# Second-layer conditioning columns: 24 of 48 moved from TensorE in the first MLP to VectorE in the second layer's attention

## The chip, the cores and the metric

The kernel runs on one core of a Trainium2 chip. Its time is the device time of one execution in microseconds (us); the figure to predict is the median of several executions. The engines are TensorE (PE, with its weight loads PEld), VectorE (DVE), ScalarE (ACT), GpSimd (POOL) and SyncE (SP), which issues most of the DMAs.

## The reference, cut to what matters

A trunk of two layers on x of 512 x 1024. From the vector c each layer makes six conditioning vectors of 1024, which scale, shift and gate its two halves:

```python
c_act = jax.nn.silu(c)
for l in range(DEPTH):                                   # DEPTH = 2
    ada = c_act @ ada_w[l] + ada_b[l]                    # 1024 x 6144 per layer
    sh1, sc1, g1, sh2, sc2, g2 = jnp.split(ada, 6, axis=-1)
    h = modulate(x, sh1, sc1)
    y = even_mixer(h, ...) if l % 2 == 0 else diff_mixer(h, ...)
    x = layer_norm(ALPHA * x + (1.0 + g1[:, None, :]) * y, ln_g[l, 0], ln_b[l, 0])
    h = modulate(x, sh2, sc2)
    y = sq_relu_mlp(h, mlp_w1[l], mlp_w2[l])
    x = layer_norm(ALPHA * x + (1.0 + g2[:, None, :]) * y, ln_g[l, 1], ln_b[l, 1])
```

`diff_mixer` projects h to queries, keys and values for 8 heads, takes two causal softmaxes per head, subtracts them, multiplies by the values, normalises and projects out. `sq_relu_mlp` is `square(relu(h @ w1)) @ w2`. All is float32.

## The kernel before, in words

The kernel keeps a conditioning vector as columns of 128 values: layer l has 48 columns m, eight for each of the six vectors, in the tile `adac[:, l, m]`. Columns 0 to 23 are sh1, sc1 and g1; columns 24 to 47 are sh2, sc2 and g2, which are first needed behind the layer's attention. A column needs 512 KB of weights, and they come by one load, like every other weight block.

All weights pass through one `Stream`. It is a list of items in a fixed order, each with a source of 512 KB in DRAM. A free "raw" buffer is given to the next item in the list, and SyncE loads it. `process` works the items off in the same order and hands the raw buffer on. A weight item is split into a high and a low float32r part (ScalarE copies the high part, line 265, and VectorE or GpSimd subtracts, line 266), which needs a free "slot" for the result. A conditioning item needs no slot. `get(item)` processes all items up to the one wanted; `pump(n)` processes up to n if a slot is there. Matmuls use three products of high and low parts (lines 350 to 352).

A conditioning item is handled in `prepare`, in one of three ways. Where `ada_pe(l, m)` holds, two items make a pair on TensorE (`ada_pair`): 8 float32 matmuls with 32 equal weight columns (line 422; each takes two instructions), a scalar copy of the result, two matmuls that bring it into column form (line 427), and an addition of the bias. Otherwise VectorE multiplies the raw block with the activated c and sums along the row (line 250, one instruction and the read of its accumulator), or GpSimd multiplies and ScalarE sums (lines 247 and 248). Now all 48 columns of layer 1 go by TensorE, spread evenly by `some` over the items of layer 0's MLP (`mlp_items`), a new one after most of its weight items.

The order of the work is written out in Python; a scheduler then places the instructions on their engines by that order as a priority, and an instruction whose inputs and buffers are there may go ahead of an earlier one that waits.

Around the change, in order: layer 0's MLP. It runs 13 groups; a group makes seven products of the first matrix (`products`, one VectorE addition at line 913 each group) between eight units of the second (`gemm2`). Then the LN of layer 0 (`ln_a`, `ln_b`, VectorE, GpSimd, ScalarE and transposes), which writes the four accumulators to DRAM (`axd`) and frees them. Then `odd`, the second layer's attention. It first projects the values: two halves of 512 columns, each for four row tiles t, each a sum over four weight items `v half c` of two blocks (24 matmuls per half and row tile). The results go to two banks "mm" of PSUM in turn. A slot is freed when t = 3 has used it, and one `pump` follows each of these. There are five slots; v00 to v03 and v10 hold them while the first half runs. Then head by head: a projection of queries and keys (items `qk`), and the softmax pipeline over 32 units (line 1681 and following). In this stretch the stream has two raw buffers. Four buffers with the tag "u4" hold the accumulators; in `odd` two of them become `V`, and the others are first used again when the residual is read back from `axd` (line 1765). Behind the heads `layer` runs the output projection, the LN and the second MLP.

Of the kernel before, what the change touches and what calls it, by code (L numbers as in the profile page):

```python
# [9 lines left out]
F32 = mybir.dt.float32  # L10
# [96 lines left out]
class Stream:  # L107
# [130 lines left out]
    def prepare(self, it):  # L238
        k, nc = self.k, self.k.nc
        n = it.n  # L240
        raw = it.raw[0][:, :n]
        if it.ada is not None:
            l, m = it.ada
            if not k.ada_pe(l, m):
                acc = k.adac[:, l, m:m + 1]
                if bool(16 <= m < 48) != ((l, m) in PLAN["ax"]):
                    nc.gpsimd.tensor_tensor(out=raw, in0=raw, in1=k.cact, op=ALU.mult)
                    nc.scalar.activation(out=raw, in_=raw, func=AF.Copy, scale=0.5, accum_out=acc)
                else:
                    nc.vector.scalar_tensor_tensor(out=raw, in0=raw, scalar=0.5, in1=k.cact, op0=ALU.mult,  # L250
                                                   op1=ALU.mult, accum_out=acc)
            elif m % 2:
                k.ada_pair(l, m - 1, self.held.raw[0], raw)
        else:
            kind = [c for c in self.kinds(it) if self.slots[c]][0]
            it.slot, it.kind = self.slots[kind].pop(0), kind
            hi, lo = it.slot
            if it.scale is not None:
                g = it.scale()
                w = 1024  # L260
                for c in range(0, n, w):
                    (nc.vector if it.name in PLAN["sc"] else nc.gpsimd).tensor_tensor(out=raw[:, c:c + w], in0=raw[:, c:c + w], in1=g[:, c:c + w], op=ALU.mult)
            for c in hi.pieces(n, {}.get(k.phase, 1024)):
                w = c.stop - c.start
                nc.scalar.copy(out=hi.cols(c.start, w), in_=raw[:, c])  # L265
                getattr(nc, ("vector", "gpsimd")[PLAN["lo"][it.name]] if it.name in PLAN["lo"] else k.lo_engine).tensor_sub(out=lo.cols(c.start, w), in0=raw[:, c], in1=f32(hi.cols(c.start, w)))  # L266
# [60 lines left out]
class Trunk:  # L327
# [80 lines left out]

    def ada_pe(self, l, m):

        return l > 0 or m >= 40

    def ada_src(self, l, m):
        return self.a["ada_p"][8 + m if l else m - 40] if self.ada_pe(l, m) else self.a["ada_w"][m]

    def ada_pair(self, l, m, r0, r1):

# [333 lines left out]
    def mlp_items(self, l):  # L751
        a, st = self.a, self.st
        def ada(n, mark=None):
            for _ in range(min(n, len(left))):
                l2, m = left.pop(0)
                self.last_ada = st.add(self.ada_src(l2, m), ada=(l2, m))
                if mark:
                    self.last_ada.after = lambda: self.marks[mark]
# [10 lines left out]
            ada((0, 0, 0, 0, 8, 0, 0, 0)[f], None)  # L769
        if left or l == 0 and 16 < 24:  # L770
            self.gate_ada = self.last_ada
        left = [(1, m) for m in range(48 - sum((0, 0, 0, 0, 0, 0, 0, 0)))] if l == 0 else []
        p0, p1 = 8, 54
        count = [0]

        def some():
            count[0] += 1
            ada(len(left) - (48 - sum((0, 0, 0, 0, 0, 0, 0, 0))) * max(0, min(p1 - p0, p1 - count[0])) // (p1 - p0) if left else 0)
        self.xd[l] = [self.DR.tile([128, 1024], F32, name=f"xd{l}{t}") for t in range(4)]
        for g, fs in enumerate(self.groups):  # L780
            if g == 13:
# [796 lines left out]
    def odd_items(self):  # L1578
        st, a = self.st, self.a
        I = self.I = {}  # L1580
        left = list(range(48 - sum((0, 0, 0, 0, 0, 0, 0, 0)), 48))
        for half in range(2):
            for c in range(4):
                I["v", half, c] = st.add(a["od_v"][half, c])
        for h in range(8):
            for m in range(2):
                I["qk", h, m] = st.add(a["od_qk"][h, m])
                I["qk", h, m].name = f"qk{h}{m}"
            for _ in range((0, 0, 0, 0, 0, 0, 0, 0)[h]):
                self.ada1 = st.add(self.ada_src(1, left[0]), ada=(1, left.pop(0)))  # L1590
        for k in range(8):
            I["oo", k] = st.add(a["od_out"][k], scale=lambda: self.gate.get((1, 0)))
            I["oo", k].name = f"oo{k}"

    def odd(self):
# [11 lines left out]
        for half in range(2):  # L1607
            V[half] = [self.s4() if half else B.tile([128, 1024], F32, tag="u4", bufs=4, name="V") for _ in range(2)]
            for t in range(4):
                ts = slice(128 * t, 128 * t + 128)  # L1610
                if half == 0 and t == 2:
                    self.tail()
                ps = self.bank("mm")
                for c in range(4):
                    w = st.get(I["v", half, c])
# [160 lines left out]
    def layer(self, l):  # L1776
# [3 lines left out]
            st.slots["x"].append(tuple(Part(*[self.s2(g, F32R) for _ in range(2)]) for g in (("q", "q"), ("k", "k"), ("q", "q"), ("k", "kl"))[s]))  # L1780
        until = st.items.index(self.I1["v", 0, 0]) if l == 0 else len(st.items)
        st.raws += [(self.s4(), until) for s in range(4)]
        if l and sum((0, 0, 0, 0, 0, 0, 0, 0)):
            st.get(self.ada1)
        self.site = 2 * l
        rows = self.ln_rows(l, 0, False)
        self.new_hT()
# [72 lines left out]
def layout(i):  # L1860
    c = np.ascontiguousarray
    i = {k: np.asarray(v) for k, v in i.items()}
    f = {}
# [7 lines left out]
    dec = 512 - (16 * np.arange(NDEC)[None, :] + 15 - np.arange(16)[:, None])  # L1871
    f["onehot"] = c(np.concatenate([onehot(511 - np.arange(NVEC)), onehot(dec.ravel())], 1))
    f["cT"] = c(i["c"].reshape(8, 128).T)
    f["ada_w"] = c(i["ada_w"][0, :, :5120].reshape(1024, 40, 128).transpose(1, 2, 0))
    p = i["ada_w"].reshape(2, 2, 4, 128, 24, 256).transpose(0, 4, 1, 3, 2, 5).reshape(96, 128, 1024)
    f["ada_p"] = c(p[40:])
    f["ada_b"] = c(i["ada_b"].reshape(2, 48, 128).transpose(2, 0, 1))
    f["lnc"] = c(np.stack([i["ln_g"], i["ln_b"]]).reshape(2, 4, 8, 128).transpose(3, 0, 1, 2))

# [50 lines left out]
```

## Time and profile before

| | us |
|---|---|
| median of 3 runs | 1438.86 (1437.71 to 1439.1) |
| the profiled execution | 1441.48 |
| its span, first to last instruction | 1439.4 |
| TensorE busy | 1338.4 (93%) |
| VectorE busy | 1141.7 (79%) |
| ScalarE busy | 659.8 (46%) |
| GpSimd busy | 579.8 (40%) |

The profile is one execution recorded by the chip's profiler. Times in a view of the timeline are us from the start of the span. Matmuls overlap, so an instruction's own duration is longer than the step from one to the next. A releaser in brackets is what ended an engine's idle time, with the length of that idle time ahead of it. The granted clock is a share of TensorE's full clock.

### The profile page before, as it was taken

The page shows a single profiled execution, that of the slowest core. Times are in us where ns is not written, and L with a number is a line of the kernel's source. Part 1 is how long each engine was busy: PE and PEld are TensorE (multiplying, and loading weights), DVE is VectorE, ACT ScalarE, POOL GpSimd, SP SyncE. Part 2 cuts the span into 40 slices and gives each one's busy share as a digit, 9 for nine tenths or more (in the row PEclk, how much of TensorE's full clock was granted, in tenths as well). Part 3 has the DMA queues.
Part 4 walks back from the last instruction along what each step waited for, and adds up shares of the span by engine and source line. Part 5 has one row for each costly group of instructions (what it writes and reads, how often), then busy time and mean ns, then how long its engine had stood idle before and what let it go on. Part 6 is the DMA issues. An engine that isn't in the chain of part 4 may idle for free.

```text
span 1439.4 us, 22546 instructions
## 1 busy us (share of the span) xinstructions
PE 1338.4 (93%) x8286; PEld 1123.1 (78%) x8286; DVE 1141.7 (79%) x2186; ACT 659.8 (46%) x1412; POOL 579.8 (40%) x432
## 2 busy tenths in 40 slices
PE   6979799998899999999999799999979899999985
PEld 4868676676589888888887687887769789999974
DVE  7778979667569778877789925788976997888898
ACT  3555465746365423333332536776565443333321
POOL 1423577626432444444453721124164533122234
PEclk9989999899999999999999999999989999999997
DMA  9834323313731554544542442332450233323311
GB/s 353 288 116 142 116 89 118 119 58 118 263 117 46 175 191 162 183 169 161 191 161 94 144 164 88 103 103 76 152 163 6 91 100 118 106 72 117 117 59 59
DMA packets 58657, 189.52 MB, mean 132 GB/s; under 512 B 7794, under 2 KB 8498, under 8 KB 58548
## 3 DMA queue, kind: packets, MB, share of 16 engines
q1 hardware_dynamic: 55840, 184.67, 38.0%
q10 hardware_dynamic: 2708, 3.42, 0.7%
q8 instruction: 65, 1.06, 0.3%
q14 instruction: 44, 0.36, 0.1%
HBM read 178.42 MB, written 9.64 MB: 131 GB/s over the span
## 4 chain that ended last, share of the span: by engine, by line
PE 70%; DVE 19%; DMA 4%; issue 3%; ACT 2%; POOL 1%; DVEq 0%; SPq 0%; ACTq 0%; POOLq 0%
PE ps_mm L350 9%; PE ps_mm L351 9%; PE ps_mm L352 9%; PE ps_o L350 4%; PE ps_o L351 4%; PE ps_o L352 4%; PE ps_s L351 3%; PE ps_s L350 3%; PE ps_s L352 3%; PE ps_t L350 2%; PE ps_t L352 2%; PE ps_t L351 2%; PE ps_t L1486 2%; PE ps_s L504 2%; DVE u L738 2%
## 5 line engine op out<-in xcount | busy, mean ns | idle before, releaser
L350 PE MATMUL ps_mm<-hT,b 128*128 128x256 f32 (+1 forms) x560 | 188.9, 339 | 16.9 <-ACT b L265 13.2
L351 PE MATMUL ps_mm<-hT,b 128*128 128x256 f32 (+1 forms) x560 | 188.5, 337 | 5.2 <-DVE hT L724 5.1
L352 PE MATMUL ps_mm<-hT,b 128*128 128x256 f32 (+1 forms) x560 | 187.8, 336 | 1.8 <-DVE b L220 1.8
L350 PEld LDWEIGHTS ps_mm<-hT,b 128*128 128x128 f32 x560 | 107.6, 192 | 31.9 <-ACT b L265 13.2
L351 PEld LDWEIGHTS ps_mm<-hT,b 128*128 128x128 f32 x560 | 107.8, 193 | 17.8 <-DVE hT L724 5.6
L220 POOL TENSOR_TENSOR b<-s,b 128x512 fp32r<-128x512 f32 x33 | 46.6, 1415 | 184.6 <-ACT b L219 181.2
L517 ACT ACTIVATE z<-z,st 128x128 f32<-128x128 f32 (+3 forms) x160 | 89.3, 559 | 67.2 <-DVE st L514 61.3
L903 POOL TENSOR_TENSOR ot<-z,ot 128x512 fp32r<-128x512 f32 x39 | 61.3, 1573 | 142.0 <-ACT ot L902 128.4
L352 PEld LDWEIGHTS ps_mm<-hT,b 128*128 128x128 f32 x560 | 107.5, 192 | 11.4 <-DVE b L220 2.0
L350 PE MATMUL ps_o<-b,ot 128*128 128x512 f32 x251 | 101.2, 403 | 3.9 <-ACT b L265 2.2
L351 PE MATMUL ps_o<-b,ot 128*128 128x512 f32 x251 | 99.5, 397 | 3.0 <-DVE b L266 3.0
L738 DVE TENSOR_TENSOR u<-ps_o,u 128x512 f32<-128x512 f32 x121 | 82.4, 681 | 21.6 <-PE ps_o L352 21.2
L352 PE MATMUL ps_o<-b,ot 128*128 128x512 f32 x251 | 98.8, 394 | 0.0
L514 DVE CUSTOM_DVE_ANT_0 z<-ps_s,g 128x128 f32<-128x128 f32 (+3 forms) x160 | 75.0, 484 | 25.8 <-PE ps_s L505 23.6
L265 ACT CAST b<-raw 128x1024 fp32r<-128x1024 f32 (+1 forms) x62 | 64.5, 1043 | 65.9 <-issue 16.7
L266 DVE TENSOR_TENSOR b<-s,b 128x1024 fp32r<-128x1024 f32 x47 | 70.4, 1501 | 18.3 <-ACT b L265 17.9
L265 ACT CAST b<-s 128x1024 fp32r<-128x1024 f32 x47 | 49.1, 1049 | 77.6 <-DMA s<-mlp_w 18.9
L266 DVE TENSOR_TENSOR b<-raw,b 128x1024 fp32r<-128x1024 f32 (+1 forms) x42 | 56.7, 1349 | 33.1 <-ACT b L265 32.9
L350 PE MATMUL ps_s<-b,ot 128*128 128x512 f32 x181 | 72.4, 400 | 0.0
L738 DVE TENSOR_TENSOR u<-ps_s,u 128x512 f32<-128x512 f32 x87 | 59.3, 682 | 15.9 <-PE ps_s L352 15.6
L351 PE MATMUL ps_s<-b,ot 128*128 128x512 f32 x181 | 71.7, 396 | 0.0
L352 PE MATMUL ps_s<-b,ot 128*128 128x512 f32 x181 | 71.4, 394 | 0.0
(472 smaller groups left out, 4244.1 us busy)
## 6 DMA issues: line engine op xcount, KB each, us to landing
s<-mlp_w SPq DMA_DIRECT2D x55, 512.0 KB
s<-ada_p SPq DMA_DIRECT2D x39, 512.0 KB
s<-mlp_wp SPq DMA_DIRECT2D x33, 512.0 KB
raw<-ada_w SPq DMA_DIRECT2D x23, 512.0 KB
raw<-mlp_w SPq DMA_DIRECT2D x21, 512.0 KB
raw<-mlp_wp SPq DMA_DIRECT2D x19, 512.0 KB
early<-ada_w SPq DMA_DIRECT2D x17, 512.0 KB
raw<-ada_p SPq DMA_DIRECT2D x17, 512.0 KB
```

The source lines that it names most:

```text
L220: (nc.gpsimd if PLAN["sl"][it.l][n] else nc.vector).tensor_tensor(out=lo, in0=src, in1=f32(hi), op=ALU.subtract)
L265: nc.scalar.copy(out=hi.cols(c.start, w), in_=raw[:, c])
L266: getattr(nc, ("vector", "gpsimd")[PLAN["lo"][it.name]] if it.name in PLAN["lo"] else k.lo_engine).tensor_sub(out=lo.cols(c.start, w), in0 ...
L350: mm(ps, lhsT=l[0], rhs=r[0], start=start, stop=False)
L351: mm(ps, lhsT=l[0], rhs=r[1], start=False, stop=False)
L352: mm(ps, lhsT=l[1], rhs=r[0], start=False, stop=stop)
L504: mm(ps, lhsT=q[:, qs], rhs=k[0][:, ks], start=start, stop=False)
L514: i = nc.vector.tensor_tensor_reduce(out=z[:, :w], in0=ps, in1=bias, scale=-1.0, scalar=3e38, op0=ALU.add, op1=ALU.min, accum_out=st[:, m: ...
L517: j = nc.scalar.activation(out=z[:, :w], in_=z[:, :w], func=AF.Exp, scale=-1.0, bias=st[:, m:m + 1], accum_out=st[:, 2 + m:3 + m])
L738: self.nc.vector.tensor_add(out=u[:, sl], in0=ps, in1=u[:, sl])
L903: (nc.gpsimd if PLAN["hl"][l][f % 2] else nc.vector).tensor_tensor(out=hl[:, c0:c1], in0=r[:, c0:c1], in1=f32(hh[:, c0:c1]), op=ALU.subtract)
L1486: self.nc.tensor.transpose(t[:, 128 * j:128 * j + 128], z[:, 128 * j:128 * j + 128], self.ident)
```

## The change

Layer 1's columns 24 to 47 are no longer pairs on TensorE in layer 0's MLP. The 24 items go into the list of the second layer's attention: four behind each of the four value weights of the second half, and two behind the query and key weights of each of heads 1 to 4. They are done on VectorE (line 250). The stream gets two more raw buffers of the tag "u4" from the start of the value projection until the weights of head 3 are issued. Before the output projection the bias is added to the three vectors. The remaining 24 items of layer 1 (columns 0 to 23) stay pairs and are spread over the same length of the MLP. The weights of the 24 columns are laid out in DRAM in the form that VectorE reads.

```diff
-                if bool(16 <= m < 48) != ((l, m) in PLAN["ax"]):
+                if bool(l == 0 and 16 <= m < 48) != ((l, m) in PLAN["ax"]):
                     nc.gpsimd.tensor_tensor(out=raw, in0=raw, in1=k.cact, op=ALU.mult)
                     nc.scalar.activation(out=raw, in_=raw, func=AF.Copy, scale=0.5, accum_out=acc)
                 else:
...
     def ada_pe(self, l, m):
-        return l > 0 or m >= 40
+        return m < 24 if l else m >= 40
...
-        left = [(1, m) for m in range(48 - sum((0, 0, 0, 0, 0, 0, 0, 0)))] if l == 0 else []
+        left = [(1, m) for m in range(24)] if l == 0 else []
...
-            ada(len(left) - (48 - sum((0, 0, 0, 0, 0, 0, 0, 0))) * max(0, min(p1 - p0, p1 - count[0])) // (p1 - p0) if left else 0)
+            ada(len(left) - 24 * max(0, min(p1 - p0, p1 - count[0])) // (p1 - p0) if left else 0)
...
     def odd_items(self):
-        left = list(range(48 - sum((0, 0, 0, 0, 0, 0, 0, 0)), 48))
+        left = list(range(24, 48))
+
+        def some(n):
+            for m in left[:n]:
+                self.ada1 = st.add(self.ada_src(1, m), ada=(1, m))
+            del left[:n]
         for half in range(2):
             for c in range(4):
                 I["v", half, c] = st.add(a["od_v"][half, c])
+                some((0, 4)[half])
         for h in range(8):
             for m in range(2):
                 I["qk", h, m] = st.add(a["od_qk"][h, m])
                 I["qk", h, m].name = f"qk{h}{m}"
-            for _ in range((0, 0, 0, 0, 0, 0, 0, 0)[h]):
-                self.ada1 = st.add(self.ada_src(1, left[0]), ada=(1, left.pop(0)))
+            some((0, 2, 2, 2, 2, 0, 0, 0)[h])
...
+                if half == 0 and t == 0:
+                    until = st.items.index(I["qk", 3, 0])
+                    st.raws += [(B.tile([128, 1024], F32, tag="u4", bufs=4, name="early"), until) for _ in range(2)]
                 ps = self.bank("mm")
...
-        if l and sum((0, 0, 0, 0, 0, 0, 0, 0)):
+        if l:
             st.get(self.ada1)
+            for sp in range(3, 6):
+                self.ada_bias(1, sp)
```

## Rows read from the trace of the kernel before

**Rows 1.** The page: busy time, moved bytes in 40 slices, chain.

```profile
PE 1338.4 (93%) x8286; PEld 1123.1 (78%) x8286; DVE 1141.7 (79%) x2186; ACT 659.8 (46%) x1412; POOL 579.8 (40%) x432
...
GB/s 353 288 116 142 116 89 118 119 58 118 263 117 46 175 191 162 183 169 161 191 161 94 144 164 88 103 103 76 152 163 6 91 100 118 106 72 117 117 59 59
...
PE 70%; DVE 19%; DMA 4%; issue 3%; ACT 2%; POOL 1%; DVEq 0%; SPq 0%; ACTq 0%; POOLq 0%
```

**Rows 2.** Windows: length, busy per engine, granted clock, DMA share, GB/s.

```profile
463.00:762.00 299.00, 298.22 (x2079) 251.31 (x2078) 235.91 (x325) 103.35 (x177) 136.68 (x86) 1.00 0.48 172
1131.00:1389.00 258.00, 257.59 (x1601) 231.37 (x1600) 225.11 (x328) 94.00 (x152) 74.78 (x50) 1.00 0.31 103
813.00:835.00 22.00, 18.86 (x91) 15.30 (x90) 14.77 (x17) 10.34 (x21) 10.75 (x7) 1.00 0.56 188
835.00:858.00 23.00, 23.00 (x110) 19.26 (x109) 4.26 (x5) 5.97 (x7) 4.76 (x2) 1.00 0.43 149
900.00:980.00 80.00, 79.58 (x434) 67.37 (x433) 63.40 (x187) 58.71 (x163) 19.38 (x22) 1.00 0.33 99
```

**Rows 3.** Timeline of TensorE around one pair: start, duration, instruction.

```profile
561.62 0.28 PE L351 MATMUL ps_mm<-k,b 128*128 128x256 f32 x1
561.84 1.07 PE L422 MATMUL ps_s<-s,ccol 128*32 128x256 f32 x16
562.84 0.39 PE L352 MATMUL ps_mm<-k,b 128*128 128x256 f32 x1
...
566.33 0.50 PE L427 MATMUL ps_s<-sel,z 128*128 128x1 f32 x4
566.69 0.36 PE L351 MATMUL ps_mm<-hT,k 128*128 128x256 f32 x1
```

**Rows 4.** Line 913 in the first and in the second MLP.

```profile
L913 DVE TENSOR_TENSOR z<-ps_mm,z x13: 410/418/425, 463.1 to 762.3; 128x256 f32<-128x256 f32 x13
...
L913 DVE TENSOR_TENSOR z<-ps_mm,z x13: 409/424/425, 1130.9 to 1389.0; 128x256 f32<-128x256 f32 x13
```

**Rows 5.** Line 250, min/median/max ns, first and last start.

```profile
L250 DVE SCALAR_TENSOR_TENSOR early<-early,cact x12: 1209/1220/1222, 7.6 to 42.4; 128x1024 f32<-128x1024 f32 x12
...
L250 DVE SCALAR_TENSOR_TENSOR raw<-raw,cact x7: 1209/1219/3086, 15.8 to 283.4; 128x1024 f32<-128x1024 f32 x7
```

**Rows 6.** Timeline of SyncE's DMA issues around the value projection.

```profile
801.41 0.33 SPq L134 DMA_DIRECT2D raw<-od_v  x1
...
824.85 3.50 SPq L1765 DMA_DIRECT2D u<-axd  x2
...
832.93 0.33 SPq L134 DMA_DIRECT2D raw<-od_v  x1
```

**Rows 7.** Timelines of ScalarE and VectorE in the value projection.

```profile
804.81 1.05 ACT L265 CAST b<-raw 128x1024 fp32r<-128x1024 f32 x1 [0.25 <-DMA raw<-od_v]
...
837.54 1.05 ACT L265 CAST b<-raw 128x1024 fp32r<-128x1024 f32 x1 [4.53 <-DMA raw<-od_v]
...
834.73 0.69 DVE L529 COPY V<-ps_mm 128x512 f32<-128x512 f32 x1 [0.46 <-PE ps_mm L352]
838.62 1.23 DVE L266 TENSOR_TENSOR b<-raw,b 128x1024 fp32r<-128x1024 f32 x1 [3.19 <-ACT b L265]
845.56 0.69 DVE L529 COPY s<-ps_mm 128x512 f32<-128x512 f32 x1 [5.71 <-PE ps_mm L352]
```

**Rows 8.** The chain in order of time, first MLP: start, length, what.

```profile
729.69 7.29 DMA s<-mlp_w
```

**Rows 9.** TensorE's timeline, and windows as in rows 2, around three gaps.

```profile
803.96 0.47 PE L713 MATMUL ps_t<-ident,ot 128*128 128x128 f32 x1 [5.37 <-DVE ot L721]
...
802.00:809.00 7.00, 5.04 (x16) 4.08 (x17) 7.00 (x12) 3.81 (x7) 5.63 (x4) 0.51 0.67 224
814.00:818.00 4.00, 0.86 (x4) 0.41 (x3) 4.00 (x4) 2.23 (x7) 4.00 (x4) 1.00 0.19 76
774.00:777.00 3.00, 0.25 (x1) 0.25 (x2) 3.00 (x3) 2.33 (x2) 0.94 (x2) 1.00 0.15 43
778.00:781.00 3.00, 3.00 (x9) 2.28 (x8) 3.00 (x8) 0.00 (x0) 0.00 (x0) 0.52 0.48 158
```

More of the change, by code (lines that the diff above doesn't have):

```diff
@@ L409, in ada_pe @@
     def ada_pe(self, l, m):
-        return l > 0 or m >= 40
+        return m < 24 if l else m >= 40
     def ada_src(self, l, m):
-        return self.a["ada_p"][8 + m if l else m - 40] if self.ada_pe(l, m) else self.a["ada_w"][m]
+        return self.a["ada_p"][8 + m if l else m - 40] if self.ada_pe(l, m) else self.a["ada_w"][m + 16 * l]
     def ada_pair(self, l, m, r0, r1):
@@ L1873, in layout @@
     f["cT"] = c(i["c"].reshape(8, 128).T)
-    f["ada_w"] = c(i["ada_w"][0, :, :5120].reshape(1024, 40, 128).transpose(1, 2, 0))
+    f["ada_w"] = c(np.concatenate([i["ada_w"][0, :, :5120], i["ada_w"][1, :, 3072:]], 1).reshape(1024, 64, 128).transpose(1, 2, 0))
     p = i["ada_w"].reshape(2, 2, 4, 128, 24, 256).transpose(0, 4, 1, 3, 2, 5).reshape(96, 128, 1024)
-    f["ada_p"] = c(p[40:])
+    f["ada_p"] = c(p[40:72])
     f["ada_b"] = c(i["ada_b"].reshape(2, 48, 128).transpose(2, 0, 1))
```

## Prediction

> **What bounds the kernel now.** I read the page first. TensorE is busy for 93% of the span, and the chain that ended last is 70% TensorE and 19% VectorE [rows 1]. That is an average, so I read the busy time by stage next [rows 2]. In the first layer's MLP (463 to 762) TensorE is busy 298.22 of 299 us at full clock while VectorE has 63 us to spare: TensorE alone bounds it. The second layer's LN and value projection run from 813 to 858. From 835 on TensorE is busy all 23 us and VectorE only 4.26. In the heads (900 to 980) TensorE is busy 79.58 of 80 us and VectorE 63.40. So a microsecond of TensorE that goes in the first MLP is won, idle TensorE in the value projection or the heads is lost, and no slack lies between these stages to swallow one or the other.
>
> **What is taken away.** Twenty-four items are twelve pairs. I read the timeline of one pair [rows 3]. The matmul before it starts at 561.62 and the one after at 562.84, where the neighbours follow each other in 0.115 us: the sixteen L422 instructions cost 1.10 us of issue. The four of L427 push the next matmul from 566.33 to 566.69: 0.36 us. A pair costs 1.46 us, twelve 17.5 us. A check from the other side: VectorE's addition of L913 comes once in each of 13 products in either MLP. It needs 299.2 us from the first to the last in the first MLP and 258.1 in the second, which does the same products and has no conditioning items [rows 4]. The difference, 41.1 us, is for 24 pairs, so 1.71 us a pair and 20.6 us for twelve; it holds whatever the pairs do to loads and banks, and also other differences between the two layers. I take **18.5 us gained**, between 17.5 and 20.6. The cover is not in doubt: with no pairs at all, in the second MLP, TensorE is still busy 257.59 of 258 us and VectorE 225.11, so VectorE does not become the bound here. The twelve scalar copies, twelve small additions and 24 loads that go with them were beside TensorE's work and count nothing.
>
> **What is added on VectorE.** Each item becomes one multiply-and-sum of L250 with its accumulator read. Nineteen of these run now, at the start of the kernel: 1.22 us at the median, 3.09 at most [rows 5]. Twenty-four take 29.3 us, 16 in the value projection, 8 in heads 1 to 4. The 16 are 19.5 us and VectorE has 18.7 idle microseconds from 835 to 858 and 7.2 before [rows 2], so the arithmetic itself is hidden. The loads are not.
>
> **The loads in the value projection.** The items go through the stream in order, and behind the weight v10 (second half, first block of rows) come four items, then v11, four items, v12, four items, v13. Block c of the second half cannot be multiplied before v1c is split, and TensorE has two accumulation banks, so it can do the first row tile and the second one in turn, and no more, while it waits. Now v11 and v12 are the next loads of the two raw buffers behind v03 and v10. With the change I number the buffers by the order in which the stream hands them out. The two new raw buffers are given to the first two items, the old ones to the third and fourth. Then v11 goes into the first new buffer behind one item; the second new buffer takes an item, another item and then v12; v13 goes into an old buffer behind three items. The new buffers are two of the four MLP accumulators, and they come free when the LN has written these to DRAM: today the reload of the residual uses the same two and is issued from 824.85 on, the second 3.17 us later (the row of two ends at 828.35, 0.33 us after its second began) at 828.02 [rows 6]. So v12 is split at the earliest at 828.0 + 3 L + 2 x 1.22 + 1.05 + 1.23, where L is a load of 512 KB from issue to landing, 1.22 an item on VectorE, 1.05 and 1.23 the two halves of a split [rows 5, 7].
>
> L by the trace: 3.4 us with no other load about (801.41 to 804.81), 4.6 with two in flight (832.93 to 837.54) [rows 6, 7], 7.29 where the chain waited for one in the busier first MLP [rows 8]. Four raw buffers will be in flight and no stage's stores with them; I take 4.6 as the nearest. Then v12 is ready at 846.5 (842.9 with 3.4, 854.6 with 7.29). TensorE wants it when both tiles have done blocks 0 and 1. The first half's last copy starts at 834.73 and the second half's second one at 845.56 [rows 7], so 48 matmuls take 10.8 us and 24 of them 5.4: at 840.1. **Idle TensorE: 6.4 us**, between 2.8 and 14.5. v11 (824.85 + 2 L + 3.5 = 837.6) is not later than TensorE gets to it at 837.4, within half a microsecond, nor is v13: if VectorE is through with the first item of its buffer at 821, v13 is split at 821 + 3 L + 2 x 1.22 + 2.28 = 839.5, ahead of v12.
>
> An idle TensorE also costs clock. Before 803.96 it had waited 5.37 us, and the granted clock of 802 to 809 is 0.51, the lower level of 1.2 GHz. Shorter gaps ended both ways: after TensorE's idle time of 774 to 777 the clock was 0.52 from 778 to 781, and in that of 814 to 818 it stayed at 1.00 [rows 9]. After the long gap some 6.3 us ran at half speed, which cost 3.1 us. A gap of 6.4 us lies on the side of the falls, but v11 may break it in two; I take 2 us, between 0 and 3.1. The Trainium skill ("TensorE: Matmul & The Clock Gate", section "HAM oscillation — how this bites in real kernels") speaks against the change here: it says that a wait for a load between bursts of matmuls lets the clock fall, so that each such wait is paid again in slow matmuls. By that rule the 3.1 us come for sure and the sum below ends 1.1 us higher; the trace shows two gaps that did so and one that did not.
>
> Before that, the third and fourth item land while VectorE works on the last LN tiles, which TensorE waits for. VectorE is busy 14.77 of 22 us there, GpSimd 10.75 beside it [rows 2]. Two items of 1.22 us can hold up the LN between 0 and 6.2 us (two at 3.09); I take 1.5. The remaining four items and the loads of the first head's weights fall under the 10.8 us of the last two row tiles and the 10.9 us of that head's projections: 0, and up to 4.6 if one load stood in the open.
>
> **The heads.** Eight items are 9.8 us on VectorE, which has 16.6 idle us from 900 to 980. They have lower priority than the softmax, but an item that has begun holds what comes next for 1.22 us. Between 0 and 9.8 us; I take 3 with the three small bias additions ahead of the output projection, nearer to nothing because TensorE never idles there now [rows 2].
>
> **Sum:** -18.5 + 6.4 + 2 + 1.5 + 3 = -5.6 us. The profiled execution took 1441.48 us (span 1439.4), 2.6 over the median 1438.86 of the runs. So 1435.9 as that one, and **1433.3 us** as the median.
>
> **Rivals.** *The ring of loads is the bound* (slower). If loads take 7.29 us with four in flight, v12 is ready at 854.6, TensorE idles 14.5 us and pays 3.1 in clock: -18.5 + 14.5 + 3.1 + 1.5 + 3 = +3.6, 1442.5 us. It decides from L = 6.1 on, where the sum is 0 (each us of L counts three times; the clock at its full price). For it: the wait of 7.29 in the first MLP. Against it: v13's load took 4.6 now, in a stretch that moved 149 GB/s [rows 2]; the ring asks for four loads in some 6 us, 350 GB/s, and the first slice of the page reaches 353 [rows 1]. *The ring costs next to nothing*: loads of 3.4 us, a gap of 2.8 without a fall of the clock, LN and heads as above: -18.5 + 2.8 + 4.5 = -11.2, 1427.7 us. For it: a load does take 3.4 by itself. Against it: four will share the bus. *The heads become VectorE's*: all 9.8 us are paid: -5.6 + 6.8 = +1.2, 1440.1 us. For it: VectorE is at 79% there; against it, 16.6 idle us. *The pairs were hidden anyway*, so that the first MLP gives 5 us instead of 18.5: +7.9, 1446.8 us. Rows 4 speak against it.
>
> **Chances.** Forecast 0.50 (its own range 1429 to 1438), ring 0.17, ring for nothing 0.18, heads 0.10, hidden pairs 0.05. A measurement of this kernel tells 0.2%, 2.9 us, from no change. Faster by more: 0.42 of the forecast's 0.50 and all of the 0.18, 0.60. Within: 0.08, 0.05 of the ring, 0.07 of the heads, 0.20. Slower: 0.12 of the ring, 0.03, 0.05, 0.20. Range: from a little under the cheap ring to a little over the dear one, 1426 to 1444.
>
> **What will show it.** The distance between first and last L913 in the first MLP: 279 to 282 us if the first step holds. TensorE's second half of the value projection: a gap before block 2 that ends with VectorE's half of a split, whose load was issued behind two items in the same buffer; its length against 6.4, and the granted clock behind it. The start of the first head's projection against the end of the first MLP: later by some 10 us relative to now. VectorE's idle time in heads 1 to 4, and TensorE's. The forecast is wrong if no gap stands in the second half, if there are several, or if the first MLP shrinks by other than 17.5 to 20.6 us.

## The result and the profile after

The changed kernel takes **1449.12 us** in the median of 6 executions (1444.91 to 1452.59), the kernel before 1438.85 beside it: a ratio of 1.0068, 95% interval 1.0052 to 1.0085. The change makes the kernel 0.7% slower. Forecast were 1433.3 us, 1426 to 1444, and faster: wrong in sign and outside the range. The profiled execution took 1451.53 us, its span 1449.7.

The page, to be held against [rows 1]: TensorE has 9.5 us less work, yet the chain has moved from it to VectorE and to DMA.

```profile
PE 1328.9 (92%) x8046; PEld 1118.8 (77%) x8046; DVE 1174.4 (81%) x2225; ACT 656.2 (45%) x1400; POOL 581.0 (40%) x432
...
PE 62%; DVE 23%; DMA 7%; issue 4%; ACT 3%; POOL 2%; DVEq 0%; ACTq 0%; POOLq 0%; SPq 0%
```

Windows of the changed kernel, columns as in [rows 2]: the first MLP, the value projection's second half, what follows up to the first softmax, its slow part, and the later heads with the output projection up to the LN.

```profile
465.00:748.00 283.00, 280.84 (x1847) 243.16 (x1846) 235.30 (x309) 99.76 (x164) 137.68 (x86) 1.00 0.41 138
825.00:848.00 23.00, 22.54 (x104) 18.66 (x102) 15.88 (x25) 5.30 (x7) 2.39 (x1) 1.00 0.85 290
848.00:875.00 27.00, 22.54 (x91) 17.97 (x92) 18.54 (x24) 11.64 (x17) 7.08 (x3) 0.87 0.73 248
851.00:859.00 8.00, 5.62 (x14) 4.51 (x15) 6.26 (x7) 2.57 (x3) 3.78 (x2) 0.57 0.78 264
947.00:1046.00 99.00, 88.11 (x470) 73.49 (x469) 82.91 (x241) 61.79 (x180) 30.52 (x25) 0.97 0.34 104
```

The same stretch of the kernel before as the last row, from the first softmax maximum of head 4 to the LN's first statistics in either kernel:

```profile
945.70:1034.80 89.10, 84.27 (x462) 70.15 (x461) 80.28 (x237) 56.66 (x164) 30.80 (x25) 1.00 0.35 107
```

The reader sees a second half of the value projection without a gap (22.54 of 23 us), which is where one was forecast, and two stretches behind it with 4.5 and 10.9 idle us and a lower clock, where none was forecast.

To place the differences, in this kernel and in the experiments e1 to e19 of the next section, I cut every profile at five instructions and use the distances between their starts, in us: **MLP**, first to last L913 of the first MLP [rows 4]; **LN and V**, from there to the first matmul of the gate row, which stands behind the value projection; **first head**, from there to the first softmax maximum; **heads**, from there to the first L913 of the second MLP (heads, output projection, LN). "Last item" is the start of the last conditioning item on VectorE or GpSimd. The ratio is to the kernel before, run on the same chip.

| kernel | MLP | LN and V | first head | heads | last item | ratio (95%) |
|---|---|---|---|---|---|---|
| before | 299.2 | 93.9 | 19.0 | 255.7 | | 1 |
| changed | 283.4 | 98.5 | 27.6 | 266.1 | 904 | 1.0068 (1.0052 to 1.0085) |
| e1 | 284.5 | 97.3 | 19.0 | 256.7 | | 0.9926 (0.9896 to 0.9955) |
| e7 | 285.2 | 99.1 | 24.3 | 256.2 | 844 | 0.9979 (0.9958 to 1.0001) |
| e10 | 287.1 | 113.8 | 19.9 | 256.8 | 841 | 1.0029 (1.0012 to 1.0047) |
| e17 | 286.7 | 96.0 | 24.2 | 256.6 | 863 | 0.9981 (0.9963 to 0.9999) |
| e18 | 284.2 | 99.6 | 26.3 | 256.6 | 865 | 0.9985 (0.9966 to 1.0005) |
| e5 | 317.3 | 100.0 | 19.0 | 255.2 | 758 | 1.0158 (1.0130 to 1.0186) |
| e14 | 307.1 | 99.8 | 19.0 | 255.2 | 743 | 1.0086 (1.0055 to 1.0118) |
| e6 | 286.1 | 107.1 | 25.5 | 259.4 | 912 | 1.0051 (1.0027 to 1.0075) |
| e15 | 286.7 | 114.8 | 20.6 | 260.0 | 915 | 1.0086 (1.0053 to 1.0118) |
| e9 | 286.2 | 112.5 | 26.9 | 261.9 | 917 | 1.0152 (1.0107 to 1.0198) |
| e16 | 285.7 | 96.4 | 26.2 | 263.1 | 887 | 1.0011 (0.9984 to 1.0037) |
| e2 | 289.2 | 102.4 | 26.0 | 264.3 | 905 | 1.0087 (1.0055 to 1.0119) |
| e8 | 285.1 | 96.7 | 21.4 | 266.6 | 900 | 1.0011 (0.9988 to 1.0034) |
| e19 | 286.5 | 99.0 | 27.3 | 267.5 | 883 | 1.0077 (1.0053 to 1.0102) |
| e11 | 287.9 | 97.3 | 19.1 | 267.8 | 904 | 0.9976 (0.9959 to 0.9993) |
| e4 | 286.4 | 97.1 | 25.8 | 274.9 | 947 | 1.0110 (1.0080 to 1.0141) |

Each row is one profile; a kernel's executions spread by some 10 us, so a distance is read against the others of its column and a verdict from the ratios. The profile of e11 is that of the longest of its ten executions, 8.1 us above their median, and that of e9 the shortest of its four, 6.8 us below.

### The profile page after: what moved, and what is told of

It reads as the page before. It is cut to its first block, busy times and chain, and to the rows that moved or that the text cites. A ratio compares the mean times of both kernels' runs of the same rounds, so it can differ in the third digit from the quotient of the medians.

```text
span 1449.7 us, 22069 instructions
## 1 busy us (share of the span) xinstructions
PE 1328.9 (92%) x8046; PEld 1118.8 (77%) x8046; DVE 1174.4 (81%) x2225; ACT 656.2 (45%) x1400; POOL 581.0 (40%) x432
## 4 chain that ended last, share of the span: by engine, by line
PE 62%; DVE 23%; DMA 7%; issue 4%; ACT 3%; POOL 2%; DVEq 0%; ACTq 0%; POOLq 0%; SPq 0%
PE ps_mm L350 8%; PE ps_mm L352 7%; PE ps_mm L351 7%; PE ps_o L350 4%; PE ps_o L351 4%; PE ps_o L352 4%; PE ps_s L350 3%; PE ps_s L351 3%; PE ps_s L352 3%; PE ps_t L350 2%; DVE b L266 2%; PE ps_t L352 2%; PE ps_t L351 2%; DMA s<-ada_p 2%; DVE u L738 2%
## 5 line engine op out<-in xcount | busy, mean ns | idle before, releaser
L350 PE MATMUL ps_mm<-hT,b 128*128 128x256 f32 (+1 forms) x560 | 190.4, 342 | 20.9 <-ACT b L265 13.3
L352 PEld LDWEIGHTS ps_mm<-hT,b 128*128 128x128 f32 x560 | 108.4, 194 | 13.1 <-DVE b L220 2.0
L265 ACT CAST b<-raw 128x1024 fp32r<-128x1024 f32 (+1 forms) x67 | 69.8, 1044 | 79.5 <-issue 15.9
L351 PE MATMUL ps_o<-b,ot 128*128 128x512 f32 x251 | 99.8, 398 | 0.0
L738 DVE TENSOR_TENSOR u<-ps_o,u 128x512 f32<-128x512 f32 x121 | 82.2, 680 | 19.7 <-PE ps_o L352 19.4
L266 DVE TENSOR_TENSOR b<-raw,b 128x1024 fp32r<-128x1024 f32 (+1 forms) x49 | 71.6, 1461 | 15.8 <-ACT b L265 15.7
L219 ACT CAST b<-s 128x512 fp32r<-128x512 f32 x78 | 47.6, 619 | 74.8 <-PE ps_mm L351 45.4
L738 DVE TENSOR_TENSOR u<-ps_s,u 128x512 f32<-128x512 f32 x87 | 59.2, 680 | 11.8 <-PE ps_s L352 11.6
L1673 POOL TENSOR_SCALAR z<-z,st,lf 128x128 f32<-128x128 f32 (+3 forms) x32 | 19.8, 618 | 120.7 <-DVE st L524 103.7
```

The source lines that it names most:

```text
L219: nc.scalar.copy(out=hi, in_=src)
L350: mm(ps, lhsT=l[0], rhs=r[0], start=start, stop=False)
L351: mm(ps, lhsT=l[0], rhs=r[1], start=False, stop=False)
L352: mm(ps, lhsT=l[1], rhs=r[0], start=False, stop=stop)
L738: self.nc.vector.tensor_add(out=u[:, sl], in0=ps, in1=u[:, sl])
L1673: j = (nc.vector if ("o", units[n][1]) in PLAN["s1"] else nc.gpsimd).tensor_scalar(out=z1[:, :w], in0=z1[:, :w], scalar1=st[:, 5:6], scala ...
```

## The experiments

All edits are made to the changed kernel.

**e1, e7, e8: one part at a time.** e1 leaves the 24 columns out (a copy of the bias stands for them), e7 makes only the 16 of the value projection, e8 only the 8 of the heads.

```diff
-                some((0, 4)[half])                      # e1, e8
-            some((0, 2, 2, 2, 2, 0, 0, 0)[h])           # e1, e7
-                    st.raws += [(B.tile(... name="early"), until) for _ in range(2)]   # e1, e8
```

> The 24 columns are not computed at all (their biases stand in for them); no items and no extra buffers in the second layer's attention. Accounting theory: the whole loss lies behind the first MLP and comes from the added items and buffers, so the 16 us that the first MLP gained stay: 1423 us, between 1421 and 1426. Rival (the changed program is ordered differently everywhere, and the last head and output projection lose some 8 us by that alone): 1430 to 1433.

> The 16 items of the value projection stay with their two extra buffers; the 8 of heads 1 to 4 are not computed (biases in their place). Theory 'each item costs what VectorE needs, wherever it stands': 16 x 1.1 over the 1430 without items: 1446 to 1449. Rival 'VectorE's idle time in the projection hides most; the heads pay': 1437 to 1441.

> Only the 8 items of heads 1 to 4, with the two raw buffers of before; the 16 of the value projection are not computed (biases in their place). From 26.8 us for 24 items in the heads, 1.1 each: 1430 + 9 = 1439 (1436 to 1441). Rival 'the first few are free, the heads have 16.6 us of idle VectorE': 1430 to 1433.

The removal alone is worth 0.74%, 10.6 us, and not 18.5. The 16 items cost 0.5% of the kernel and the 8 items 0.85%; together 1.4%, the distance from e1 to the changed kernel. So the fewer items, those of the heads, seem to have the larger price; the intervals of e7 and e8 overlap a little.

**e2: the two extra buffers from another tag** (`self.s4()`), so that the accumulators stay out of it.

> The changed kernel, but its two extra raw buffers are of the tag s4 (free in the value projection) instead of u4. Theory 'the extra buffers take the accumulators that V needs, V's first copy waits from 799 to 811 and holds a PSUM bank': that wait goes, the projection starts some 5 us earlier, 1443 us (1441 to 1446). Rival 'VectorE's items inside the LN chain make the delay': no change, 1447 to 1451.

1.0087: no gain. **e15: the extra buffers asked for at the fourth row tile**, behind V's own.

```diff
-                if half == 0 and t == 0:
+                if half == 0 and t == 3:
```

> The changed kernel, with its two extra raw buffers asked for at the first half's fourth row tile rather than at its first, behind the V tiles. Theory (the predicted gap did not come because the extra buffers got the two accumulators that were freed first, at 796 and 801, and V waited instead, at no cost): now V's first copy is back near 800, the extra buffers' first loads are issued near 825 to 828, v12 is late, and TensorE idles 3 to 9 us before the third block of the second half; gate row 3 to 10 us later than in the changed kernel, 1452 to 1460 us (1.009 to 1.014). Rival (the load time in the ring is short enough, and the gap would not have come anyway): gate row within 2 us of the changed kernel's, same time, 1.005 to 1.008.

Here the forecast's gap is there. TensorE, ScalarE and SyncE of e15, the instructions that end the gaps before the second and third block:

```profile
838.12 1.22 PE L350 MATMUL ps_mm<-b,hT 128*128 128x512 f32 x2 [7.37 <-ACT b L265]
...
847.33 1.22 PE L350 MATMUL ps_mm<-b,hT 128*128 128x512 f32 x2 [3.77 <-ACT b L265]
...
837.02 1.04 ACT L265 CAST b<-early 128x1024 fp32r<-128x1024 f32 x1 [2.35 <-DMA early<-od_v]
...
846.24 1.04 ACT L265 CAST b<-early 128x1024 fp32r<-128x1024 f32 x1 [8.17 <-DMA early<-od_v]
...
815.74 3.29 SPq L134 DMA_DIRECT2D early<-ada_w  x2
...
832.33 0.33 SPq L134 DMA_DIRECT2D early<-od_v  x1
...
840.50 0.33 SPq L134 DMA_DIRECT2D early<-od_v  x1
```

v11 and v12 are issued behind items in the extra buffers, and LN and V takes 16.3 us more than in the changed kernel. The first head and the heads then take 13.1 us less, and the ratio, 1.0086, can't be told from the changed kernel's. So the wait seems to have changed its place. That the third block begins at 847.3, near the forecast's 846.5, is luck: the first two loads of the extra buffers are issued 9 us earlier than it had (815.7 and 818.7), and the loads and items from there to v12 take longer. TensorE is also there earlier, so the longer gap stands before the second block, where none was forecast.

**e10: the 16 items further ahead** (6, 5, 5, 0 behind v10 to v13); the other eight columns are not computed.

```diff
-                some((0, 4)[half])
+                some((0, (6, 5, 5, 0)[c])[half])
```

> As e7_values_only (16 items in the value projection, none in the heads), but six, five and five behind v10, v11 and v12 and none behind v13. The 6 us that e7 lost against the kernel without items lay between the gate row and the first softmax. Theory 'the last four items stand in VectorE's and the raw buffers' queue before the first head's weights and before the copies that free TensorE's banks': they go, 1431 to 1434. Rival 'sixteen loads more delay the first head's weights wherever they stand, or now v11 to v13 come late': 1437 or more.

The first head is spared (19.9), but TensorE waits 1.1 us for v11 and 8.1 us for v12, and LN and V loses 14.7 us against e7: 1.0029. TensorE's gap before the third block:

```profile
843.22 1.22 PE L350 MATMUL ps_mm<-b,hT 128*128 128x512 f32 x2 [8.05 <-ACT b L265]
```

**e6, e11: the items short.** VectorE sums 64 of the 1024 elements; loads and order of the list stay. e6 has all 24 items, e11 the 8 of e8.

```diff
-                    nc.vector.scalar_tensor_tensor(out=raw, in0=raw, ...
+                    w = 64 if l else 1024
+                    nc.vector.scalar_tensor_tensor(out=raw[:, :w], in0=raw[:, :w], ...
```

> The changed kernel with all its loads, buffers and places, but each of the 24 items multiplies and sums 64 of its 1024 elements alone, so VectorE works some 0.2 us on it instead of 1.22. Theory 'the price of the items is VectorE's time' (24 x 1.22 = 29 us, 20 of which showed): the time falls to 1431 to 1436, close to the 1430 without any items. Rival 'loads, raw buffers and the order of the stream are the price': it stays at 1445 to 1450.

> As e8_eight_in_heads (8 items in heads 1 to 4 alone, 1442), with all loads, but each item sums 64 of 1024 elements. If VectorE's time is the heads' price: 1431 to 1434. If the loads and the in-order stream are: 1440 to 1443.

e6 is at 1.0051, an interval that overlaps the changed kernel's; e11 at 0.9976 against 1.0011 of e8, with the same long heads (267.8). By these ratios VectorE's time is the smaller part of the price, 0.35 of the 0.85% of e8 and 0.17 of the 1.42% of all, and neither part is clear of the noise. What is left of e11 is clear of it: it stands 0.55 and 0.92% above e12 and e13, which ran beside it on the same chip and have no item.

**e12, e13: VectorE's work without loads**, e1 with eight multiply-sums on the activated c where heads 1 to 4 are processed (1024 and 8 elements).

> The kernel without items (1430), plus 8 full-size multiply-and-sum instructions on VectorE on a tile that lies in SBUF, in the places of the 8 items and without their loads. If VectorE's time or a changed order is the price: 1439 to 1443. If the loads are: 1430 to 1433.

> As e12_heads_no_load, but the 8 instructions take 8 of 1024 elements, some 0.15 us each, and there is no load: what is left is the changed order of the program. If order alone is the price: 1438 to 1443. If it is loads or VectorE's time: 1429 to 1432.

They missed their place. The trace of e12 (count, duration, first to last start):

```profile
L192 DVE SCALAR_TENSOR_TENSOR cact<-cact x8: 1204/1216/1515, 292.9 to 310.8; 128x1024 f32<-128x1024 f32 x8
```

Nothing in the heads was needed for them, so the scheduler put them into the first layer. They say nothing of the heads. As kernels close to e1 (0.9921 and 0.9884 against 0.9926) they show that ratios can differ by 0.4% between kernels that are alike but for a few VectorE instructions in the first layer.

**e4, e16: all 24 items in heads 0 to 5; and the 8 of e8 with two more raw buffers up to the output projection.**

```diff
+                if half == 1 and t == 0:                                   # e16, on e8
+                    until = st.items.index(I["oo", 0])
+                    st.raws += [(self.s4(), until) for _ in range(2)]
```

> All 24 items stand behind the query and key weights of heads 0 to 5, four each, with the two raw buffers of before; nothing is added in the value projection. Theory 'the value projection loses 12 us, the heads 3 to 4 per eight items, the last head some 8': the 12 us come back, the heads pay 9 to 12: about 1433 us if the last head's 8 us came from the projection's delay, 1440 if the items themselves bring them. Rival 'the heads are VectorE's with 24 items': 24 x 1.22 = 29 us on VectorE, over 1448.

> The kernel with only eight items in heads 1 to 4 (16 columns not computed; 1.0011 with two raw buffers), with two further raw buffers from the start of the second half of the value projection to the output projection's weights. Theory (the eight items cost 12 us because each takes a turn of the only two raw buffers, so that every later block of query and key weights is loaded and split one turn later): with four buffers the loads run ahead, the splits come as early as in the kernel without the items, and the time falls to 1430 to 1435 (0.992 to 0.997), with only VectorE's up to 5 us left. Rival 1 (the turn is not the price, but the transfers themselves or the place of the items in the in-order list): unchanged, 0.999 to 1.003. Rival 2 (loads that come earlier collide with other traffic or hold buffers that others wait for): slower, 1.004 or more.

24 items in the heads cost most, 19 us over the kernel before there. Four buffers give what two gave, 1.0011: the turn of a buffer is not the whole price.

**e5, e9, e14: other engines and the other place.** e9 undoes line 246, so that GpSimd multiplies and ScalarE sums; e5 does it so in the first MLP, interleaved with the remaining pairs; e14 does the same on VectorE.

```diff
-                if bool(l == 0 and 16 <= m < 48) != ((l, m) in PLAN["ax"]):
+                if bool(16 <= m < 48) != ((l, m) in PLAN["ax"]):           # e5, e9
-        left = [(1, m) for m in range(24)] if l == 0 else []
+        left = [(1, 24 * j + 2 * i + o) for i in range(12) for j in range(2) for o in range(2)] if l == 0 else []   # e5, e14
```

> The 24 items stay in the first MLP, in twos behind each pair, but GpSimd multiplies and ScalarE sums (the path of lines 247 and 248) instead of TensorE; the attention is as before. Theory: TensorE bounds the first MLP and GpSimd has room (136.68 of 299 us busy, plus 24 x 2.4): the 16 us are won and nothing is lost, 1423 to 1426. Rival 'GpSimd's 2.4 us and the port it shares with VectorE slow VectorE, which then bounds the MLP': 1431 to 1436.

> The changed kernel, but its 24 items are multiplied on GpSimd and summed on ScalarE instead of VectorE; places, loads and buffers as in the changed kernel. Theory 'VectorE's time is the price' and GpSimd has room: 1436 to 1442. Rival 'GpSimd beside VectorE slows VectorE as much, and ScalarE's 1.05 us stand in the softmax': 1450 to 1460.

> The 24 columns stay in the first MLP's list, interleaved with the 24 pair items as before, but VectorE makes them (line 250); nothing of them is in the attention. Theory (the price of the change lies in its loads and items in the attention's stream, and VectorE has 63 idle us in the first MLP for 29.3 us of items): TensorE wins there what it won with the columns left out, first to last L913 near 284 us against 299.2, nothing is lost in the attention, 1428 to 1435 us (0.992 to 0.997). Rival (a 1.22 us item on VectorE in the MLP holds up what TensorE waits for, as the items of GpSimd did): TensorE idle by some us in 463 to 745, L913 from first to last 290 us or more, 1438 us or more (1.000 up). Which of these also says whether VectorE or GpSimd beside it was the trouble of the GpSimd run (1.0158).

e9 is at 1.0152, slower than the changed kernel, so GpSimd is no relief. e14's rival came: 24 items on VectorE make the MLP longer than the twelve pairs that they replace (307.1 against 299.2), though VectorE had 63 idle us. Its L913, its L250 in the MLP with the idle time ahead of it, and TensorE's waits there (total, times, longest):

```profile
L913 DVE TENSOR_TENSOR z<-ps_mm,z x13: 406/409/419, 457.4 to 764.5; 128x256 f32<-128x256 f32 x13
```

```profile
L250 DVE SCALAR_TENSOR_TENSOR s<-s,cact x17: 1208/1424/2322, 464.3 to 722.1; 128x1024 f32<-128x1024 f32 x17
...
its engine sat idle before it (us, times) until:
  DMA s<-ada_w: 16.4, 8
  DMA raw<-ada_w: 11.8, 3
```

```profile
PE ps_s L422 <- DMA s<-ada_p: 12.1, 7, 2.6
PE ps_o L350 <- DVE u L738: 3.6, 5, 1.3
```

Eleven of the 24 items stood at the head of VectorE's queue before their load had landed and kept it idle for 28.2 us, with the evacuations (L738) behind them. But the larger part of TensorE's waits, 13.5 us, is for the loads of the remaining pairs (12.1 and, from raw buffers, 1.4); some 6 us are for results of VectorE. In e5 the same loads cost it 20.9 us. The 63 idle us of VectorE were no room for 24 items and their loads.

**e17, e18, e19: items outside the stream**, in buffers of their own: one meant for each of the eight heads (e17, on e1); one behind each value tile and one in each head, the other eight columns as pairs (e18); two behind each value tile and one in each head (e19). e14, e18 and e19 compute everything, as do e2, e4, e5, e9 and e15.

```diff
+            for _ in range(plan.get(n, 0)):
+                x = B.tile([128, 1024], F32, tag="u4", bufs=4, name="early") if n < 0 else self.s4()
+                own.append((cols.pop(0), x))
+                nc.sync.dma_start(out=x, in_=self.ada_src(1, own[-1][0]))
```

> Eight items in the heads as in the kernel with only these (16 columns not computed; 1.0011), with the same 512 KB loads and the same VectorE instructions, but not in the weight stream: the loads go into buffers of their own, issued by SyncE behind a softmax step. TensorE's instructions then stand in the order that they have without any item (24 of 7343 stand elsewhere; in the stream it was some 600 in the heads). Theory (the price is the item's place in the in-order stream and the order of TensorE's instructions that follows from it, not its transfer nor VectorE's time): as without items, 0.991 to 0.995, and the distance from the gate row to the first LN as in that kernel, within 2 us. Rival (512 KB more of traffic per item in the heads is the price): 0.998 to 1.003, 8 us or more between gate row and LN.

> Whole computation: 16 of the 24 columns on VectorE outside the stream, in buffers of their own, one behind each of the eight value tiles and one in each head; the other 8 stay pairs in the first MLP (16 pairs there). Theory: eight pairs fewer give two thirds of what the removal of twelve gave (0.74% of it, so 0.5%), and the items cost nothing there: 0.993 to 0.998, faster than both kernels. Rival (loads among the value weights or in the heads cost as before): 0.999 to 1.006.

> Whole computation: all 24 columns on VectorE outside the stream, two behind each of the eight value tiles and one in each head. Here TensorE's order in the heads is again another (some 650 instructions stand elsewhere). Theory 1 (the place in the stream is the price): 0.991 to 0.997. Theory 2 (the order in which TensorE's instructions of the heads stand is the price, whatever changes it): the values cost little, the heads lose 8 to 13 us, 0.998 to 1.004. Rival (VectorE's 29 us are too much for this place): gaps on VectorE in the value projection, gate row 5 us or more behind that of the kernel without the items.

e17 missed its place as well: its buffers were free early, and all eight items ran around the first head's projection.

```profile
L1613 DVE SCALAR_TENSOR_TENSOR s<-s,cact x8: 1206/1226/3376, 841.3 to 863.4; 128x1024 f32<-128x1024 f32 x8
```

So it is no test of the heads; it shows that eight items outside the stream cost the first head 5.2 us there, as the sixteen of e7 did in it (5.3), and nothing later. The items that e18 and e19 meant for the heads ran early too, the last at 865 and 883. e18 is at 0.9985 (0.9966 to 1.0005), not to be told from before. e19 loses as the changed kernel does. No whole version beats the kernel before.

## Why the prediction was wrong

In short: the removal was put too high, the gap that was priced did not come, and the loss stands in the first head and the heads, which had been put at 0 and 3 us.

**The removal (-18.5).** The distance of L913 shrank by 15.8 us where 17.5 to 20.6 were expected:

```profile
L913 DVE TENSOR_TENSOR z<-ps_mm,z x13: 405/414/425, 464.6 to 748.0; 128x256 f32<-128x256 f32 x13
```

TensorE's busy time fell about as priced, by 17.4 us (298.22 to 280.84 in the two windows). But its idle time is 2.2 of 283 us against 0.8 of 299 before, and 2.0 of the 2.2 are waits of a remaining pair for its load. TensorE's waits in the first MLP (total, times and longest), in the changed kernel and then in e10:

```profile
PE ps_s L422 <- DMA s<-ada_p: 2.0, 4, 1.3
```

```profile
PE ps_s L422 <- DMA s<-ada_p: 5.9, 5, 1.7
```

Fifteen experiments have the same first MLP as the changed kernel. There the wait is 3.3 to 6.7 us and the distance 284.5 to 289.2, so the 15.8 us are the best case: the median of the sixteen, 286.4, gives 12.8. e18 keeps 16 pairs, waits 0.6 us and needs 284.2, no more than with 12. The step that failed is "a microsecond of TensorE that goes in the first MLP is won": part of it is waited away, for the loads of the pairs that stay. Why these come later with twelve pairs than with 24 or 16 was not tested.

More of the gain went at the stage's end: with the removal alone (e1) LN and V takes 3.4 us more. "No slack lies between these stages" was wrong. VectorE is nearly full behind the MLP, as [rows 9] already had it (774 to 777: VectorE 3.00 of 3.00), so a TensorE that is done earlier does not get on faster. The 28 us from the last L913 on, before and then e1:

```profile
762.30:790.30 28.00, 24.93 (x113) 19.95 (x112) 27.48 (x39) 7.06 (x8) 9.69 (x6) 0.94 0.29 93
```

```profile
749.00:777.00 28.00, 22.75 (x95) 17.59 (x94) 26.28 (x36) 7.04 (x9) 9.33 (x6) 0.88 0.24 81
```

TensorE idles 5.3 us in e1 and 3.1 before, at a lower clock; the LN's first statistics come 27.6 us behind the last L913 against 25.8. The rest of the 3.4 us stands in the value projection: behind the same gap of 3.1 us the clock fell in e1 (0.52 over 807.5 to 811) and not before (1.00 over 817.5 to 822). Net 10.6 us, by the ratio of e1.

**The gap before v12 (+6.4, clock +2, LN +1.5).** The step that failed is "v12 is split at the earliest at 828.0 + 3 L": it gave the extra buffers the accumulators that the residual's reload has now. SyncE of the changed kernel, against [rows 6]:

```profile
795.85 0.38 SPq L134 DMA_DIRECT2D early<-ada_w  x1
...
801.01 0.33 SPq L134 DMA_DIRECT2D early<-ada_w  x1
...
820.63 0.33 SPq L134 DMA_DIRECT2D early<-od_v  x1
```

The extra buffers are asked for ahead of V's first copy and took the two accumulators freed first. V waited instead; its first copy, in the changed kernel and then in e1:

```profile
811.12 0.58 ACT L531 COPY V<-ps_mm 128x512 f32<-128x512 f32 x1
```

```profile
802.20 0.58 ACT L531 COPY V<-ps_mm 128x512 f32<-128x512 f32 x1
```

No wait of TensorE ended with that copy, and little was lost: gate row at 846.49 against 856.24 before, as early as in e1 (846.3). With the order turned round (e15) gaps came, 7.4 and 3.8 us. The mechanism was right, its premise not. The price of the clock was high as well: of the low stretch in [rows 9], 802 to 809, some 5 us lie behind the gap that ended at 803.96, not 6.3, so it cost 2.5 us and not 3.1. LN and V cost 4.6 us over before, 3.4 of them the removal's.

**The first head (0, up to 4.6): +8.6.** The step that failed is "fall under the 10.8 us of the last two row tiles and the 10.9 us of that head's projections: 0". VectorE, ScalarE, GpSimd and TensorE of the changed kernel:

```profile
848.33 3.25 DVE L250 SCALAR_TENSOR_TENSOR raw<-raw,cact 128x1024 f32<-128x1024 f32 x1 [3.04 <-DMA raw<-ada_w]
...
852.65 0.68 DVE L529 COPY s<-ps_mm 128x512 f32<-128x512 f32 x1
...
847.03 1.04 ACT L265 CAST b<-early 128x1024 fp32r<-128x1024 f32 x1 [5.19 <-DMA early<-od_qk]
847.99 1.04 ACT L265 CAST b<-raw 128x1024 fp32r<-128x1024 f32 x1
848.93 0.58 ACT L440 COPY grow<-ps_mm 128x512 f32<-128x512 f32 x1
...
848.16 2.34 POOL L266 TENSOR_TENSOR b<-early,b 128x1024 fp32r<-128x1024 f32 x1 [5.79 <-ACT b L265]
...
849.56 1.16 PE L438 MATMUL ps_mm<-ident,adac 128*128 128x128 f32 x8 [2.02 <-ACT grow L440]
...
853.38 0.80 PE L350 MATMUL ps_mm<-hT,b 128*128 128x512 f32 x1 [2.66 <-DVE s L529]
```

An item waits 3.04 us for its load at the head of VectorE's queue and then takes 3.25 us beside GpSimd's split. The evacuation of the last value tile stands behind it, and TensorE waits 2.66 us for its bank. On ScalarE a split that waits 5.19 us for its weights holds the gate row's copy, and TensorE waits another 2.02. Then the clock falls: 0.57 over 851 to 859, close to the lower level of 1.2 GHz. So the stretch has 4.5 idle us and a clock of 0.87. I had counted items against idle time and left out what is queued behind one that waits.

**The heads (+3, 0 to 9.8): +10.4.** The place is that of the rival "the heads become VectorE's", which had 9.8, but VectorE's time is not the main cause: short items leave most of the loss (e11). Nor is the buffers' turn enough to explain it (e16). Most of it falls where no item runs. The items on VectorE behind the first MLP:

```profile
L250 DVE SCALAR_TENSOR_TENSOR raw<-raw,cact x14: 1209/1225/3255, 799.7 to 904.5; 128x1024 f32<-128x1024 f32 x14
...
L250 DVE SCALAR_TENSOR_TENSOR early<-early,cact x10: 1212/1221/3214, 805.1 to 869.7; 128x1024 f32<-128x1024 f32 x10
```

The last starts at 904.5. Head 4's first maximum is at 947.2 against 945.7 before, 1.5 us late; the LN's first statistics are at 1046.2 against 1034.8, 11.4 late. The two windows above say how: 10.9 idle us of TensorE where there were 4.8, and 3.8 us more of busy time at a clock of 0.97. The forecast had put the term near nothing "because TensorE never idles there now", read from 900 to 980; in the later heads it idled even then. One of these waits, VectorE and GpSimd before TensorE:

```profile
1028.05 2.34 DVE L392 TENSOR_TENSOR t<-t,ost 128x4 f32<-128x4 f32 x1
1030.31 1.21 DVE L266 TENSOR_TENSOR b<-raw,b 128x1024 fp32r<-128x1024 f32 x1
...
1027.88 2.48 POOL L266 TENSOR_TENSOR b<-raw,b 128x1024 fp32r<-128x1024 f32 x1 [1.57 <-ACT b L265]
...
1031.58 0.50 PE L351 MATMUL ps_mm<-b,ot 128*128 128x512 f32 x1 [2.18 <-DVE b L266]
```

Here VectorE's split of an output weight stands behind a chain of small instructions, the last of which takes 2.34 us beside GpSimd; in the kernel before TensorE waits for no split in that stretch. What differs, 120 us behind the last item, is the order in which the instructions stand in the engines' programs. I compared TensorE's in the traces: from the first softmax maximum to the second MLP, some 1360 matmuls, the kernels without an item behind 866 us (e1, e5, e7, e10, e12 to e14, e17, e18) have it as before but for 17 at most, and their heads take 255.2 to 257.1 us. In the ten others, the changed kernel among them, 290 to 473 stand out of the old order, and the heads take 259.4 to 274.9. The scheduler has another order as soon as an item falls into the heads.

Two runs come near to parting the order from the items. In e19 no item stands in the stream and the last runs at 883.3, yet from head 4's first maximum to the LN's first statistics it takes 104.0 us, 14.0 of them idle, where the kernel before takes 89.1 with 4.8:

```profile
948.10:1052.10 104.00, 89.98 (x474) 74.51 (x474) 86.02 (x243) 63.17 (x179) 31.35 (x25) 0.97 0.32 99
```

And a later stream of weights is not needed for the loss: in e16 the last load of query and key weights is issued 35.8 us behind the first softmax maximum against 54.5 before, and its heads are 7.4 us longer. Both speak for the order. But the loss goes with the item and with the order at once, and no run here changed the order alone: the cause of the largest term stays open.

**The rest of the sum.** -15.8 + 4.6 + 8.6 + 10.4 is 7.8; 1.5 lie ahead of the first L913 and 1.1 from the second MLP on, as they differ between profiles anyway: 10.4, against 10.3 between the spans (1439.4 to 1449.7). Of the rivals, "hidden pairs" had a removal of 5, too little; in the changed kernel no gap of the ring, cheap or dear, stood in the second half.

## What to carry to other kernels

An engine's idle share is room only for instructions whose data is there when their turn comes: in an in-order queue an instruction that waits for a load costs everybody who waits for what is behind it, so price it by its wait and its successors, not by its duration. The same holds where work is taken away: look at what the remaining work of that kind waits for. Before a gap is forecast from a buffer, look which request takes the buffer that comes free first. And where a scheduler orders the program, look in the trace where an added instruction really ran, and whether the order elsewhere is still the old one, before reading a time as its price.

## What the hardware showed unexpectedly

GpSimd and VectorE stretch each other: the item of 1.22 us took 3.25 beside a GpSimd split of 2.34 us, and an addition of 128x4 elements 2.34 us beside one of 2.48 (rows above). The Trainium skill ("GPSIMD Engine Reference", section "Specifications") says that GpSimd shares its SBUF interfaces with VectorE and contends with VectorE instructions that have two SBUF inputs. The trace agrees: both have two.

Clock: TensorE's gaps of 2.02 and 2.66 us end within 4 us of each other (849.56, 853.38), and the granted clock, full over 849 to 851.5, is at the lower level from 851.7 on, inside the second gap:

```profile
849.00:851.50 2.50, 1.16 (x8) 0.97 (x8) 2.50 (x1) 0.94 (x3) 1.50 (x1) 1.00 0.97 395
851.70:858.40 6.70, 5.02 (x12) 4.00 (x13) 5.56 (x5) 1.94 (x3) 3.18 (x2) 0.50 0.79 262
```

The one idle stretch that the forecast priced was never there, but the clock fell here, and by a little in the later heads (0.97 over 947 to 1046), at shorter ones that it had not.
